# A two-layer fp32 trunk on one core: fp32 output projections, squares and reciprocals on TensorE, down operands summed earlier

## The chip, the core and the metric

The kernel runs on one core of a Trainium2 chip. The core has a matrix engine (TensorE, PE in the profile, with its weight loads as PEld), VectorE (DVE), ScalarE (ACT), GpSimd (POOL) and SyncE (SP, which here issues DMAs); matmuls write to PSUM banks, all other work is between PSUM and SBUF, and DMAs move data to and from DRAM. The metric is the time of one execution on the device in microseconds.

## The reference

Two decoder layers over x of 1024 positions by 1024 features, all in float32. Cut to what matters here:

```python
for layer in range(DEPTH):
    h = rms_norm(x, norm_g)
    # layer 0: 8 MLA heads (softmax) and 8 stick-breaking heads; layer 1: 16 forgetting-attention heads (softmax)
    x = x + (even_mixer(h, positions, *mp) if layer % 2 == 0 else odd_mixer(h, *mp))   # ends in merge_heads(o) @ w_o
    x = x + swiglu(rms_norm(x, f_norm), w_gate, w_up, w_down)

def rms_norm(x, g):
    return x * lax.rsqrt(jnp.mean(x * x, axis=-1, keepdims=True) + EPS) * g
def swiglu(h, w_gate, w_up, w_down):            # 1024 -> 2816 -> 1024
    return (jax.nn.silu(h @ w_gate) * (h @ w_up)) @ w_down
```

Each softmax divides a head's weighted sum of values by the sum of its weights.

## The kernel before

Activations lie transposed, 128 features by 1024 positions (two halves, hf, of 512). **A large product is done in blocks of 2 x 2** by Winograd's form of Strassen's scheme: seven products, taken in the order 1, 6, 5, 7, 2, 4, 3 (`ORDER`), of sums of the four weight blocks (A) with sums of the four activation blocks (X: X11, T2, T1, X12', X21, T4, X22). `pair` (L252) does one pair of 128-row output blocks over nk blocks of the contracted dimension. It loads four raw weight tiles, makes the sums S1 to S4 on POOL (`gadd`, L165), and splits each operand in two fp32r parts: `split` (L153) copies the high part on ACT (L155) and subtracts on DVE to get the low part (L156, or L159 with a sign). Each fp32 product of one block is then three fp32r matmuls, high x high, high x low, low x high, all 128 x 128 weights on 128 x 512. `xadds`/`xsplit` (L232 to L250) make the X sums on POOL and split them, into tiles named xo.

The seven products go to PSUM banks ba, bb, bc. They come back in three ways: product by product with a copy r1 (L321) and two sums U2, U3 (L323, L326); **product by product with an accumulator** (`acc`, L298: nine DVE adds of a bank into an SBUF tile); or **k by k** (`kmajor`, L335, its matmuls at L342), which starts as soon as the first X block is there and needs the weights of all products at once.

**The stages of a layer.** The normalized input's projection; attention head by head (`Heads`, scores St, exponentials p, products with values O at L995); output projection `out_proj` (L1114, four pairs of nk = 4, p = 0 k by k and 1 to 3 with accumulators); eleven gate and eleven up pairs (`ffn`, L1144); down in chunks of 3, 3, 3 and 2 blocks with four pairs each.

**End of attention.** `finish` (L1001) evacuates O: 64 rows of values to a tile o, row 64 (the weights' sum) to a tile dn by ACT (L1012). The reciprocals of each pair of heads go by DMA on POOL's queue: dn to DRAM (rd), back as 128 columns (rc), reciprocal on DVE (L1026), to DRAM (rr), back broadcast to 64 rows (rb), then a multiply on POOL (`scale`, L1035). `out_x` (L1101) loads the heads' results as X of the output projection; for the last pair it uses o where it lies.

**Norms.** `absorb` (L374) takes the outputs of a projection or of down, scales them by the next norm's gain, prepares them as X of the next stage and sums their squares: for the norm in front of the gate/up of layer 0 and others by adds on DVE (L162), or, for those in `PESQ` = (0, 16), by fp32 matmuls with a column block of 64 ones into one bank (L413).

**FFN.** `fu` (L1167 to L1177) multiplies up by the gate's result s, on POOL for three of four tiles, and writes s to DRAM (hS, four writes of 256 KB a pair of blocks). For down, `hadds` loads them (two tiles hld of 512 KB per block), makes the X sums on POOL and splits them; the first two of chunk 0 (`PRE`) are made before the last up pair.

The program is written in this order, and each engine takes its instructions in order; the order on each engine is decided when the program is built, from due times within fixed rings of buffers (`BUFS`: b4 28, T 6, wo 5, raw 6, S 3). SP issues nearly all loads and stores, so a store that waits for its data holds the loads behind it.

Of the kernel before, what the change touches and what calls it, by code (L numbers as in the profile page):

```python
# [19 lines left out]
P = 128  # L20
T = 1024
# [15 lines left out]
PRE = 2  # L37
FGT = 7
LATE = (0,)
PESQ = (0, 16)  # L40
# [37 lines left out]
class Heads:  # L78
# [10 lines left out]
    def run(self, t):  # L89
# [38 lines left out]
class Trunk:  # L128
# [123 lines left out]
    def pair(self, w, nk, X, evac, first=None, acc=None):  # L252
# [20 lines left out]
        for n in ORDER:  # L273
            t = self.tl("hl" if first and n in ORDER[5:] else "wo", "wo", (P, 2, 4, P), F32R)
# [17 lines left out]
        if acc is not None:  # L292
            r = {}

            def plus(ti, hf, bank):
                if (ti, hf) not in r:
                    r[ti, hf] = acc(ti, hf)
                nc.vector.tensor_tensor(r[ti, hf], bank, r[ti, hf], ALU.add)  # L298
            prod(1, ba, True)
            plus(1, 1, ba)  # L300
            plus(1, 0, ba)
            plus(0, 1, ba)
            prod(6, bb, True)
            plus(0, 1, bb)
            prod(5, bc, True)
            plus(1, 1, bc)
            prod(7, bb, False)
            plus(1, 1, bb)
            evac(1, 1, r[1, 1])
            prod(2, ba, False)  # L310
            plus(0, 0, ba)
            evac(0, 0, r[0, 0])
            prod(4, bb, False)
            plus(1, 0, bb)
            evac(1, 0, r[1, 0])
            prod(3, bc, False)
            plus(0, 1, bc)
            evac(0, 1, r[0, 1])
            return
# [15 lines left out]
    def kmajor(self, A, X, ks, evac, r1, U2, U3):  # L335
# [3 lines left out]
        for m, k in enumerate(ks):  # L339
            for n in ORDER:  # L340
                for i, (a, b) in enumerate(((0, 0), (0, 1), (1, 0))):
                    nc.tensor.matmul(bank[n], A[n][:, a, k], X[n, k][:, b], start=m == 0 and i == 0,  # L342
                                     stop=m == len(ks) - 1 and i == 2, skip_group_check=True)
# [1022 lines left out]
```

## Time and profile before

| | us |
|---|---|
| median of 3 runs (lowest, highest) | 2813.67 (2801.68, 2820.46) |
| the profiled execution | 2817.3 |
| its span, first to last instruction | 2815.5 |
| PE busy in the span | 2622.2 |
| DVE / POOL / ACT busy | 2179.3 / 1587.7 / 1367.4 |
| mean granted clock of TensorE | 0.964 |

By time: attention of layer 0 ends about 645 us, its output projection runs to 778, gate and up to 1185, down to 1475; in layer 1 the projection lies from 1997 to 2152 and down from 2559 to the end. A matmul record is one pass as the profiler lists it; a native fp32 matmul shows as two. Busy times of an engine are the time in which at least one of its instructions ran; an engine's idle time is put down to what ended it.

### The profile page before, as it was taken

How to read it: one execution, taken by the hardware profiler on the slowest of the kernel's cores; microseconds unless marked ns; L12 is line 12 of the kernel's file. 1: busy time of each engine (PE TensorE's matmuls, PEld its weight loads, DVE VectorE, ACT ScalarE, POOL GpSimd, SP SyncE). 2: the span in 40 equal slices, each digit the busy share in tenths (PEclk: the TensorE clock that was granted, in tenths of full speed). 3: DMA queues.
4: the chain of work that ended last, by engine and by line, in shares of the span. 5: the costliest groups of instructions: out<-in, count | busy, mean ns of one | idle time of the engine just before them, and what ended most of it. 6: DMA issues, size and time to landing. Idle time of an engine off the chain costs nothing.

```text
span 2815.5 us, 35148 instructions
## 1 busy us (share of the span) xinstructions
PE 2622.2 (93%) x11422; PEld 1963.0 (70%) x11422; DVE 2179.3 (77%) x3063; ACT 1367.4 (49%) x2640; POOL 1587.7 (56%) x1355
## 2 busy tenths in 40 slices
PE   7999998997899999998999998999789999998889
PEld 3775554765678888776758866666567888886667
DVE  8777777886965555788899887999799555558987
ACT  5437775673533332343367753777544333333333
POOL 5545665135576666876565533122556666678763
PEclk9999997998999999999999999999899999999999
DMA  3466645624232222242233437666242322224222
GB/s 116 162 203 196 197 148 151 160 84 143 86 98 89 85 77 86 89 149 87 76 109 125 144 123 223 151 176 181 94 133 67 108 86 75 86 77 163 90 90 90
DMA packets 166511, 343.38 MB, mean 122 GB/s; under 512 B 20524, under 2 KB 43904, under 8 KB 166328
## 3 DMA queue, kind: packets, MB, share of 16 engines
q1 hardware_dynamic: 160888, 329.21, 37.9%
q0 software_dynamic: 5056, 11.84, 1.4%
q8 instruction: 90, 1.47, 0.2%
q14 instruction: 93, 0.76, 0.1%
q10 hardware_dynamic: 384, 0.10, 0.0%
HBM read 232.96 MB, written 108.09 MB: 121 GB/s over the span
## 4 chain that ended last, share of the span: by engine, by line
PE 63%; DVE 17%; issue 5%; ACT 5%; DMA 4%; POOL 2%; SPq 0%; DVEq 0%; ACTq 0%; POOLq 0%
PE bb L289 19%; PE bc L289 13%; PE ba L289 13%; PE O L995 5%; DVE xo L156 5%; PE St L974 4%; PE P L342 3%; DVE wo L156 3%; PE Sm L948 2%; DVE acc L298 1%; DVE R L1079 1%; DVE p L985 1%; ACT xo L155 1%; PE psu L659 1%; PE Sz L1069 1%
## 5 line engine op out<-in xcount | busy, mean ns | idle before, releaser
L289 PE MATMUL bb<-xo,wo 128*128 128x512 f32 x2970 | 746.8, 398 | 13.0 <-DVE U L323 4.6
L289 PEld LDWEIGHTS bb<-xo,wo 128*128 128x128 f32 x2970 | 560.9, 190 | 155.3 <-DVE U L323 6.6
L289 PE MATMUL ba<-xo,wo 128*128 128x512 f32 x1980 | 518.6, 406 | 38.3 <-DVE acc L298 19.8
L289 PE MATMUL bc<-xo,wo 128*128 128x512 f32 x1980 | 499.3, 398 | 11.9 <-ACT sq L409 9.4
L289 PEld LDWEIGHTS ba<-xo,wo 128*128 128x128 f32 x1980 | 381.8, 194 | 140.2 <-issue 19.1
L289 PEld LDWEIGHTS bc<-xo,wo 128*128 128x128 f32 x1980 | 373.0, 189 | 107.8 <-ACT sq L409 10.2
L155 ACT ACTIVATE wo<-S 128x512 fp32r<-128x512 f32 (+2 forms) x416 | 241.5, 586 | 413.0 <-PE bb L289 128.4
L156 DVE TENSOR_TENSOR wo<-S,wo 128x512 fp32r<-128x512 f32 (+2 forms) x416 | 381.0, 919 | 72.8 <-ACT wo L155 71.4
L165 POOL TENSOR_TENSOR S<-raw 128x512 f32<-128x512 f32 (+2 forms) x208 | 292.3, 1406 | 111.8 <-DVE wo L156 93.5
L342 PE MATMUL P<-xo,wo 128*128 128x512 f32 x966 | 270.6, 425 | 67.9 <-DVE xo L156 26.0
L995 PE MATMUL O<-p,v 128*65 128x512 f32 (+3 forms) x1152 | 302.4, 364 | 7.9 <-ACT p L984 4.2
L342 PEld LDWEIGHTS P<-xo,wo 128*128 128x128 f32 x966 | 189.7, 202 | 142.5 <-DVE xo L156 39.4
L165 POOL TENSOR_TENSOR S<-raw,S 128x512 f32<-128x512 f32 (+2 forms) x104 | 133.2, 1281 | 272.6 <-issue 153.8
L165 POOL TENSOR_TENSOR s<-s,rs 128x512 f32<-128x512 f32 x156 | 234.5, 1512 | 76.5 <-DVE wo L156 45.3
L155 ACT ACTIVATE wo<-raw 128x512 fp32r<-128x512 f32 (+2 forms) x208 | 121.8, 586 | 312.3 <-PE bb L289 187.4
L156 DVE TENSOR_TENSOR wo<-raw,wo 128x512 fp32r<-128x512 f32 (+2 forms) x208 | 197.8, 951 | 34.0 <-ACT wo L155 34.0
L995 PEld LDWEIGHTS O<-p,v 128*65 128x65 f32 x1152 | 146.9, 142 | 71.5 <-ACT p L155 11.0
L985 DVE TENSOR_TENSOR p<-E,p 128x512 fp32r<-128x512 f32 (+2 forms) x288 | 182.3, 651 | 18.3 <-ACT p L984 16.3
L981 ACT ACTIVATE E<-St 128x512 f32<-128x512 f32 (+2 forms) x288 | 147.4, 518 | 96.4 <-PE St L978 67.0
L156 DVE TENSOR_TENSOR xo<-T,xo 128x512 fp32r<-128x512 f32 x138 | 152.3, 1119 | 42.2 <-ACT xo L155 41.8
L953 DVE TENSOR_REDUCE M<-Sm 128x1 f32<-128x512 f32 (+3 forms) x288 | 152.6, 549 | 26.1 <-PE Sm L951 16.3
L165 POOL TENSOR_TENSOR S<-S,raw 128x512 f32<-128x512 f32 (+2 forms) x104 | 137.7, 1324 | 21.2 <-issue 7.7
(297 smaller groups left out, 4191.6 us busy)
## 6 DMA issues: line engine op xcount, KB each, us to landing
hS<-s SPq DMA_DIRECT2D x88, 256.0 KB
hld<-hS SPq DMA_DIRECT2D x44, 512.0 KB
raw<-in_w1in_dram SPq DMA_DIRECT2D x48, 256.0 KB
Q<-fq SPq DMA_DIRECT2D x48, 256.0 KB
K<-fk SPq DMA_DIRECT2D x48, 256.0 KB
raw<-in_w0g_dram SPq DMA_DIRECT2D x44, 256.0 KB
raw<-in_w0u_dram SPq DMA_DIRECT2D x44, 256.0 KB
raw<-in_w1g_dram SPq DMA_DIRECT2D x44, 256.0 KB
```

The lines of the kernel that those rows point to most:

```text
L155: nc.scalar.activation(hi, src, AF.Copy)
L156: nc.vector.tensor_tensor(lo, src, hi.bitcast(F32), ALU.subtract)
L165: return self.nc.gpsimd.tensor_tensor(o, a, b, op)
L289: nc.tensor.matmul(bank, A[n][:, a, k], X[n, k][:, b], start=first and m == 0, stop=m == 3 * nk - 1, skip_group_check=True)
L298: nc.vector.tensor_tensor(r[ti, hf], bank, r[ti, hf], ALU.add)
L342: nc.tensor.matmul(bank[n], A[n][:, a, k], X[n, k][:, b], start=m == 0 and i == 0, stop=m == len(ks) - 1 and i == 2, skip_group_check=True)
L948: nc.tensor.matmul(S[:, 0:e1 - c0], lhs[:, i * P:(i + 1) * P], rhs[:, c0:e1], start=True, stop=not diag, skip_group_check=True)
L953: nc.vector.tensor_reduce(M[:, m:m + 1], S[:, 0:n], AX.X, ALU.max)
L974: nc.tensor.matmul(S[:, o:H], k[:, j * P:(j + 1) * P], q[:, s:(hf + 1) * H], start=m == 0, stop=m == n - 1 and not diag, skip_group_check= ...
L981: nc.scalar.activation(E[:, o:H], S[:, o:H], AF.Exp)
L985: nc.vector.tensor_tensor(pl[:, o:H], E[:, o:H], ph[:, o:H].bitcast(F32), ALU.subtract)
L995: nc.tensor.matmul(a["O"][hf][0:VW, o:H], v[:, l], p[:, o:H], start=j == 0 and m == 0, stop=last and m == 2, skip_group_check=True)
```

## The change

Five edits.

1. The output projections use `pair32`: no operand is split, each block product is one native fp32 matmul (112 per layer). `out_x` makes its four X sums on POOL and keeps them as they are.
2. For the last two heads of layer 0's softmax heads and of layer 1's, `divide` takes the reciprocals' place over DRAM: four fp32 matmuls turn the row dn into a column block pt, DVE takes reciprocals of 128 x 4, four fp32 matmuls spread them over 64 rows (rb), and DVE multiplies. It is done for each of two heads and two halves.
3. `PESQ` is (0, 8, 16, 24): all norms sum their squares by matmul.
4. In `ffn`, the X sums T1, T2, T4 and X12' of down are made on POOL behind each up pair, and all seven operands are written to DRAM, 256 KB each. Down loads each operand (hx) in product order and splits it; all its pairs use accumulators, none goes k by k. Of `fu`'s three multiplies on POOL two move to DVE. `PRE` is gone.
5. `NAT` = (1,): product 1 of down is native fp32, with A11 and X11 unsplit.

```diff
-PRE = 2
+NAT = (1,)
-PESQ = (0, 16)
+PESQ = (0, 8, 16, 24)
...
+            for k in range(nk if n in nat else 0):
+                nc.tensor.matmul(bank, A[n][:, k], X[n, k], start=first and k == 0, stop=k == nk - 1,
+                                 skip_group_check=True)
...
+        if a["s"].keep and a["h"] >= a["s"].n - 2:
+            return self.divide(a, O, o[r:r + 64], a["dn"][64:65, cols])
...
+    def divide(self, a, O, o, dn):
+        nc = self.nc
+        pt = self.bank("pt", (P, 4), ring="sm")
+        for b in range(4):
+            nc.tensor.matmul(pt[:, b:b + 1], dn[:, b * P:(b + 1) * P], self.one[64:65, 0:1], start=True, stop=True,
+                             skip_group_check=True)
+        rc = self.tl("rd", "rc", (P, 4))
+        nc.vector.reciprocal(rc, pt)
+        rb = self.bank("rb", (64, H), ring="sm")
+        for b in range(4):
+            nc.tensor.matmul(rb[:, b * P:(b + 1) * P], rc[:, b:b + 1].broadcast_to([P, 64]), self.ident, start=True,
+                             stop=True, skip_group_check=True)
+        nc.scalar.copy(o, O[0:64])
+        nc.vector.tensor_tensor(o, o, rb, ALU.mult)
...
-        self.xprep(X, i, q[0], q[1])
+        (X11, X12), (X21, X22) = q
+        t = self.tl("b4", "T12", (P, 2, H))
+        T4 = self.tl("b4", "T4", (P, 2, H))[:, 0]
+        T1, T2 = t[:, 0], t[:, 1]
+        self.gadd(T1, X12, X11, ALU.subtract)
+        self.gadd(T2, X22, T1, ALU.subtract)
+        self.gadd(X12, X22, X12, ALU.subtract)
+        self.gadd(T4, X21, T2, ALU.subtract)
+        for n, x in ((1, X11), (6, T2), (5, T1), (7, X12), (2, X21), (4, T4), (3, X22)):
+            X[n, i] = x
+
+    def pair32(self, w, X, evac, first=None, acc=None):
...
+        def mm(bank, n, k, start, stop):
+            self.nc.tensor.matmul(bank, A[n][:, k], X[n, k], start=start, stop=stop, skip_group_check=True)
...
-                    u = self.tl("T", "u")
+                    last = (ti, hf) != (1, 1)
+                    u = bank if last else add
                     nc.vector.tensor_tensor(u, bank, add, ALU.add)
-                    self.gadd(s, s, u, ALU.mult)
-                nc.sync.dma_start(hS[2 * i + ti, :, hf * H:(hf + 1) * H], s)
+                    (nc.vector if last else nc.gpsimd).tensor_tensor(s, u, s, ALU.mult)
+                if (ti, hf) != (0, 1):
+                    keep(i, 1 + 2 * ti - ti * (1 - hf), s)
...
+            T1, T2, T4 = [self.tl("T", n) for n in ("T1", "T2", "T4")]
...
+            for n, t in ((5, T1), (6, T2), (7, X12), (4, T4)):
+                keep(i, n, t)
...
-            for i in range(nk):
-                self.xsplit(X, i, early.pop(0) if early else hadds(base + i))
+            for n in ORDER:
+                for i in range(nk):
+                    if n in NAT:
+                        if i % 2 == 0:
+                            two = self.tl("b4", "hx2", (P, 2, H))
+                        X[n, i] = two[:, i % 2]
+                        self.load(X[n, i], hS[base + i, n - 1])
+                    else:
+                        t = self.tl("T", "hx")
+                        self.load(t, hS[base + i, n - 1])
+                        X[n, i] = self.tl("b4", "xo", (P, 2, H), F32R)
+                        self.split(X[n, i][:, 0], X[n, i][:, 1], t)
```

Three places in the order that the edits make. First TensorE at the end of layer 0's attention, behind the last scores, before the change (O: products with values; P: the projection's first pair, three fp32r matmuls to a block):

```order
L978 MATMUL St<-maskkb,identb 128x256
L995 MATMUL O_6212<-p,v 65x512 x4
L995 MATMUL O_6211<-p,v 65x256 x2
L342 MATMUL P_6464<-xo,wo 128x512 x6
L995 MATMUL O_6211<-p,v 65x256
L342 MATMUL P_6466<-xo,wo 128x512 x3
L342 MATMUL P_6465<-xo,wo 128x512 x4
L342 MATMUL P_6466<-xo,wo 128x512
L342 MATMUL P_6465<-xo,wo 128x512 x2
L342 MATMUL P_6466<-xo,wo 128x512 x2
L995 MATMUL O_6212<-p,v 65x512 x2
L342 MATMUL P_6467<-xo,wo 128x512 x6
```

and with it (P at L1172 are native matmuls, one to a block; pt is the divide's):

```order
L1172 MATMUL P_6396<-T_6359,raw 128x512
L1172 MATMUL P_6392<-T_6048,S_6382 128x512
L1172 MATMUL P_6392<-T_6224,S_6382 128x512
L1172 MATMUL P_6392<-T_6358,S_6382 128x512
L1011 MATMUL O_6213<-p,v 65x256 x2
L1172 MATMUL P_6394<-o_6044,S_6383 128x512
L1172 MATMUL P_6394<-o_6220,S_6383 128x512
L1172 MATMUL P_6394<-o_6354,S_6383 128x512
L1011 MATMUL O_6213<-p,v 65x256 x4
L1046 MATMUL pt<-oner,dn 128x1 x4
L1172 MATMUL P_6393<-T_6048,S_6382 128x512
L1172 MATMUL P_6393<-T_6224,S_6382 128x512
```

The products with values now have native matmuls between them whose operands are raw weights and sums, and pt stands behind the last of them.

Second SP ahead of layer 0's down, before (s: results of an up pair, those from s_10263 on of the last; hld: the loads of down's chunk 0 that are still out):

```order
L1177 DMA hS0_7220<-s_10008 128x512
L168 DMA raw_10550<-in_w0d0_dram 128x384
L168 DMA raw_10552<-in_w0d0_dram 128x384
L168 DMA hld_10514<-hS0_7220 128x1024
L168 DMA hld_10516<-hS0_7220 128x1024
L168 DMA raw_10676<-in_w0d0_dram 128x384
L168 DMA acc_10659<-x1_102 128x512
L168 DMA acc_10663<-x1_102 128x512
L168 DMA raw_10678<-in_w0d0_dram 128x384
L168 DMA raw_10680<-in_w0d0_dram 128x384
L168 DMA raw_10682<-in_w0d0_dram 128x384
L1177 DMA hS0_7220<-s_10263 128x512
```

and with the change, from the last up pair's first result on (hx: loads of down's operands):

```order
L1220 DMA hS0_6845<-s_9958 128x512
L172 DMA raw_10364<-in_w0d0_dram 128x384
L1220 DMA hS0_6845<-s_9962 128x512
L172 DMA raw_10468<-in_w0d0_dram 128x384
L1220 DMA hS0_6845<-s_9979 128x512
L172 DMA raw_10470<-in_w0d0_dram 128x384
L1220 DMA hS0_6845<-T1_10141 128x512
L172 DMA hx_10157<-hS0_6845 128x512
L172 DMA hx_10167<-hS0_6845 128x512
L1220 DMA hS0_6845<-T2_10142 128x512
L172 DMA hx_10162<-hS0_6845 128x512
L172 DMA hx_10172<-hS0_6845 128x512
```

All loads of chunk 0 stood ahead of the last up pair's writes; now its first split operands are loaded behind the write of T1, a sum made of that pair's results.

Third DVE in down of layer 0, shortly ahead of the start of a chunk, before (xo: operand splits of the next chunk, wo: weight splits, acc: accumulates):

```order
L298 TENSOR_TENSOR acc_10967<-bb,acc_10967 128x512
L156 TENSOR_TENSOR xo<-hld,xo 128x512
L156 TENSOR_TENSOR wo<-S_10927,wo 128x384
L156 TENSOR_TENSOR xo<-hld,xo 128x512
L156 TENSOR_TENSOR xo<-T_11069,xo 128x512
L298 TENSOR_TENSOR acc_10962<-bc,acc_10962 128x512
L156 TENSOR_TENSOR xo<-T_11067,xo 128x512
L156 TENSOR_TENSOR xo<-hld,xo 128x512
L156 TENSOR_TENSOR wo<-raw,wo 128x384
L156 TENSOR_TENSOR xo<-hld,xo 128x512
L298 TENSOR_TENSOR acc_10967<-ba,acc_10967 128x512
L156 TENSOR_TENSOR xo<-T_11072,xo 128x512
```

and with the change:

```order
L331 TENSOR_TENSOR acc_10622<-bb,acc_10622 128x512
L160 TENSOR_TENSOR xo<-hx,xo 128x512
L160 TENSOR_TENSOR wo<-S_10591,wo 128x384
L160 TENSOR_TENSOR xo<-hx,xo 128x512 x2
L331 TENSOR_TENSOR acc_10617<-bc,acc_10617 128x512
L160 TENSOR_TENSOR xo<-hx,xo 128x512 x2
L160 TENSOR_TENSOR wo<-S_10791,wo 128x384
L160 TENSOR_TENSOR xo<-hx,xo 128x512
L331 TENSOR_TENSOR acc_10622<-ba,acc_10622 128x512
L160 TENSOR_TENSOR xo<-hx,xo 128x512
L160 TENSOR_TENSOR wo<-S_10789,wo 128x384
```

In both, the next chunk's operand splits stand between the accumulates of the pair that runs; now they come from hx, in product order.

## Rows read from the trace of the kernel before

**Rows 1.** Page, part 1: busy us (share of the span) xinstructions.

```profile
PE 2622.2 (93%) x11422; PEld 1963.0 (70%) x11422; DVE 2179.3 (77%) x3063; ACT 1367.4 (49%) x2640; POOL 1587.7 (56%) x1355
```

**Rows 2.** Windows: stretch, length, busy (count) of PE PEld DVE ACT POOL, clock, DMA.

```profile
778.00:1185.00 407.00, 402.99 (x1719) 323.37 (x1718) 239.24 (x281) 132.58 (x221) 289.70 (x199) 1.00 0.28 88
818.00:857.00 39.00, 39.00 (x168) 31.37 (x168) 20.93 (x26) 11.99 (x20) 25.90 (x19) 1.00 0.34 108
623.00:778.00 155.00, 124.56 (x474) 94.60 (x474) 130.57 (x158) 72.66 (x130) 89.92 (x62) 0.88 0.34 107
1997.00:2152.00 155.00, 125.00 (x473) 94.20 (x473) 134.03 (x159) 73.63 (x133) 88.35 (x64) 0.88 0.34 107
1185.00:1475.00 290.00, 267.49 (x1070) 200.15 (x1069) 263.23 (x362) 130.11 (x252) 186.89 (x140) 0.97 0.32 105
2559.00:2816.00 257.00, 230.64 (x951) 180.95 (x949) 219.98 (x321) 87.97 (x177) 149.75 (x117) 0.97 0.32 108
1252.00:1321.00 69.00, 61.90 (x256) 48.44 (x255) 61.88 (x84) 25.79 (x51) 44.83 (x33) 0.98 0.28 88
```

**Rows 3.** Chain of waits at 2055 us: start, us, what.

```profile
2059.59 2.80 PE ba L289 x12
2062.39 2.80 PE bb L289 x12
```

**Rows 4.** The same windows' sum over 600:623, 1970:1997, 778:800, 2152:2175.

```profile
sum 95.00, PE 86.70 PEld 64.02 DVE 82.13 ACT 56.35 POOL 57.77; mean PE 21.68 PEld 16.00 DVE 20.53 ACT 14.09 POOL 14.44
```

**Rows 5.** What PE waited for in 623:778: total us, times, longest.

```profile
PE P L342 <- DVE xo L156: 11.1, 4, 4.4
```

**Rows 6.** DVE groups by form: count, busy us, mean ns, idle before.

```profile
L156 DVE TENSOR_TENSOR wo<-S,wo 128x512 fp32r<-128x512 f32 x288 | 283.8, 987 | 68.4 <-ACT wo L155 67.0
...
L156 DVE TENSOR_TENSOR xo<-hld,xo 128x512 fp32r<-128x512 f32 x88 | 83.1, 953 | 0.0
L156 DVE TENSOR_TENSOR wo<-S,wo 128x384 fp32r<-128x384 f32 x96 | 80.5, 844 | 3.0 <-ACT wo L155 3.0
...
L298 DVE TENSOR_TENSOR acc<-ba,acc 128x512 f32<-128x512 f32 x96 | 61.6, 678 | 3.1 <-PE ba L289 3.0
```

**Rows 7.** Timeline of PE at 116 us: start, us, line, operation, count.

```profile
116.46 1.02 PE L492 MATMUL psn<-sqf,oner 128*128 128x512 f32 x2
116.92 2.65 PE L289 MATMUL bb<-xo,wo 128*128 128x512 f32 x9
119.41 1.02 PE L492 MATMUL psn<-sqf,oner 128*128 128x512 f32 x2
```

**Rows 8.** Timeline of PE at 1460 us, squares.

```profile
1460.09 1.07 PE L413 MATMUL pmr<-sq,oner 128*64 128x512 f32 x2
1461.10 1.90 PE L342 MATMUL P<-xo,wo 128*128 128x512 f32 x7
1462.92 1.08 PE L413 MATMUL pmr<-sq,oner 128*64 128x512 f32 x4
1463.93 1.43 PE L342 MATMUL P<-xo,wo 128*128 128x512 f32 x5
```

**Rows 9.** Timeline of PE at 229 us, small fp32 matmuls.

```profile
229.79 0.60 PE L1095 MATMUL Sa<-cst,A 128*128 128x128 f32 x4
```

**Rows 10.** Chain of waits, reciprocals of layer 1.

```profile
2020.25 3.47 DMA rd<-dn
...
2024.30 2.09 DMA rc<-rd
...
2030.01 5.26 DMA rb<-rr
```

**Rows 11.** Tile hld: duration ns min/median/max, first and last start.

```profile
L156 DVE TENSOR_TENSOR xo<-hld,xo x88: 670/678/1805, 1164.0 to 2769.5; 128x512 fp32r<-128x512 f32 x88
L168 SPq DMA_DIRECT2D hld<-hS x44: 319/327/433, 806.8 to 2720.7; - x44
L165 POOL TENSOR_TENSOR T<-hld x22: 1282/1607/1766, 1148.7 to 2725.2; 128x512 f32<-128x512 f32 x22
```

More of the change, by code (lines that the diff above doesn't have):

```diff
@@ L250, in xsplit, with pair @@
             self.split(t[:, 0], t[:, 1], s)
[L252 removed]
+    def pair(self, w, nk, X, evac, first=None, acc=None, nat=()):
         nc = self.nc
@@ L292, in pair @@
         if acc is not None:
[L293 to L319, printed above, removed]
+            return self.nmajor(prod, evac, acc)
+        ba, bb, bc = [self.bank(n, ring=n) for n in ("ba", "bb", "bc")]
         prod(1, ba, True)
@@ L333, in pair, with nmajor, plus, kmajor @@
         evac(0, 1, bc, U2)
-    def kmajor(self, A, X, ks, evac, r1, U2, U3):
+    def nmajor(self, prod, evac, acc):
+        nc = self.nc
+        ba, bb, bc = [self.bank(n, ring=n) for n in ("ba", "bb", "bc")]
+        r = {}
+        def plus(ti, hf, bank):
+            if (ti, hf) not in r:
+                r[ti, hf] = acc(ti, hf)
+            nc.vector.tensor_tensor(r[ti, hf], bank, r[ti, hf], ALU.add)
+        prod(1, ba, True)
+        plus(1, 1, ba)
+        plus(1, 0, ba)
+        plus(0, 1, ba)
+        prod(6, bb, True)
+        plus(0, 1, bb)
+        prod(5, bc, True)
+        plus(1, 1, bc)
+        prod(7, bb, False)
+        plus(1, 1, bb)
+        evac(1, 1, r[1, 1])
+        prod(2, ba, False)
+        plus(0, 0, ba)
+        evac(0, 0, r[0, 0])
+        prod(4, bb, False)
+        plus(1, 0, bb)
+        evac(1, 0, r[1, 0])
+        prod(3, bc, False)
+        plus(0, 1, bc)
+        evac(0, 1, r[0, 1])
+    def kmajor(self, mm, ks, evac, r1, U2, U3):
         nc = self.nc
@@ L340, in kmajor @@
             for n in ORDER:
-                for i, (a, b) in enumerate(((0, 0), (0, 1), (1, 0))):
-                    nc.tensor.matmul(bank[n], A[n][:, a, k], X[n, k][:, b], start=m == 0 and i == 0,
-                                     stop=m == len(ks) - 1 and i == 2, skip_group_check=True)
+                mm(bank[n], n, k, m == 0, m == len(ks) - 1)
         nc.scalar.copy(r1, bank[1])
@@ L1139, in out_proj @@
             if p == 0:
-                self.pair(w[p], 4, X, f, first=order)
+                self.pair32(w[p], X, f, first=order)
             else:
-                self.pair(w[p], 4, X, done, acc=start)
+                self.pair32(w[p], X, done, acc=start)
             self.absorb(e, p, [[got[t, h] for h in range(2)] for t in range(2)])
```

70 lines of the change are left out of this document (44 added, 26 removed).

## Prediction

> **What bounds the kernel now.** I start on the page: TensorE (PE) is busy 93% of the span, no other engine over 77% [rows 1]. Time can be won only by taking matmul time away or by filling the 7%, and the windows by stage say where that is. In the gate and up stage PE is busy 402.99 of 407 us, and one steady pair of 39.00 us holds 168 matmul records [rows 2]. The chain of waits, in a stretch where PE is the chain, gives 2.80 us for 12 of these records, 0.2333 us each [rows 3]; 168 x 0.2333 = 39.2 us, so nothing is lost there, and VectorE (DVE) and GpSimd (POOL) have room. I apply the same price to the other stages of [rows 2], as window minus records x 0.2333: output projection of layer 0 155 - 474 x 0.2333 = 44.4 us lost, of layer 1 155 - 473 x 0.2333 = 44.6, down of layer 0 290 - 1070 x 0.2333 = 40.4, down of layer 1 257 - 951 x 0.2333 = 35.1 (about 6 of it the output's tail, an estimate). Together 164 us, the whole prize. It counts a lower granted clock (0.88 in the projections, 0.97 in down) as lost; I take it to come back with the idle time around it. The last 23 to 27 us of both attentions and the first 22 of both FFNs add 95.00 - 86.70 = 8 us of plain idle time [rows 4].
>
> The waits name who holds PE in the projection: above all the fp32r operands xo from DVE [rows 5]. In down DVE is busy 263 of 290 us [rows 2], and most of that is operand splits: one takes 0.84 to 0.99 us on average, an accumulate out of PSUM 0.68 [rows 6].
>
> **What the change adds to PE.**
> Native fp32: 224 matmuls in the two projections and 88 in down take the place of three fp32r records each (0.70 us). The trace has native matmuls of the same shape, the norm's psn: from 116.46 to 119.41 us there are 2.95 us, with nine fp32r records inside, 2.95 - 9 x 0.2333 = 0.85 [rows 7]. So 312 x (0.85 - 0.70) = 47 us. Bounds: 0.70 (nothing) and the 1.01 us of the squares below (97 us). I take 0.85, as it has the shape.
> Squares: 32 sums move from DVE to TensorE. One square holds PE from 1460.09 to 1461.10, 1.01 us; two side by side from 1462.92 to 1463.93, again 1.01 [rows 8]. By the order the squares stand in 48 such lots after and 24 before: 24 us more. Eight fp32r records of the norms go, 8 x 0.2333 = 2. Net 22 us.
> Divides: eight in the program, each 8 tiny fp32 matmuls, 16 records. A small fp32 record takes 0.15 us [rows 9]: 2.4 us each, 19 in all. Bounds 1 us (were they to overlap) and 3.5 (a wait for the copy and the reciprocal in each), 8 to 28.
> Sum: 47 + 22 + 19 = 88 us more matmul time. The change pays only if it wins back more than 88 of the 164 and 8.
>
> **What it wins.**
> Projections. All operand splits go (28 of X and 28 of the weights per layer), and with them most of DVE's 131 us in 155 [rows 2]. The reciprocals' way over DRAM, 15 us from the issue of rd to the landing of rb [rows 10], becomes a copy, a reciprocal and 8 matmuls on PE's own queue. By the order, natives with operands that are ready (raw weights, POOL sums of earlier head pairs) stand between the last PV products, so PE can run on. Late next: pt, which waits for the last PV and the copy of dn; behind it the multiply and POOL's four sums on that result (1.28 us each at the least [rows 11], two in line before product 6); and the norm's chain at the FFN's start, which stays. I leave 8 us of each 44.5 and win 73; bounds 60, were the POOL sums the bound at each step, and 81.
> Ends of attention and first pairs: 8 us, since natives and squares can stand in the gaps.
> Down. Per chunk of three, DVE drops three X splits of 21 and four weight splits of 28, 3 x 0.95 + 4 x 0.84 = 6.2 us, and gains two accumulates (9 in the place of 7 at the first pair), 1.4 us: from 62 us in one chunk [rows 2] to 57, while PE's work is 4 x (18 x 0.70 + 3 x 0.85) = 60.6. POOL loses 12 sums and 4 accumulates per chunk, so the splits, whose least time is 0.67 us and whose longest 1.81 [rows 11], should come nearer the first. Inside a chunk DVE is then no longer last. What stays is the starts. In layer 0 the first operands of chunk 0 stand on SP behind the writes of the last gate/up pair, T1's among them, and T1 needs the last evacuation; before, they came early. I count an add and a multiply of 0.68 us, T1's 1.6, two issues of 0.33 [rows 11], the landing, and a split on two engines of 0.68 each: 5.0 us and the landing, for which the nearest rows are 2.09 and 5.26 [rows 10]: 7 to 10, and I take 9. Two chunk boundaries cost 3 each: by the order DVE has 18 X splits, 19 weight splits and 27 accumulates in the three pairs ahead of one, at 0.85, 0.7 and 0.68 us 47 us against PE's 45.5. The last chunk, where absorb shares DVE, 7. So 22 of 40.4 stay and 18 are won. Layer 1: 9, 6, 3 for its last chunk and the output's 6, 24 of 35.1; won 11.
> Gate and up. POOL gets four sums a pair, loses two multiplies and, once, the eight sums of the early X: with 1.6 us for each [rows 11], 290 + 10 x 2 x 1.6 - 8 x 1.6 = 309 us of 407; DVE gets two multiplies of 0.68 a pair, 14 us on 239. Seven writes of 256 KB a pair for four are 0.75 MB in 39 us, 20 GB/s on 108, at a DMA share of 0.34 [rows 2]. PE hides all of it: price 0. Without that cover the two extra POOL operations cost their 3.2 us a pair, 70 in both layers.
> Won: 73 + 8 + 18 + 11 = 110. Net -22: 2817.3 - 22 = 2795 against the profiled execution's own time, which lies 3.6 us above the median of the runs; on the median's level **2792 us**.
>
> **The rivals.**
> Faster: the waits in down all but vanish, because DVE falls well under PE. For it: 57 us or fewer against 60.6, with POOL half empty. Against it: by the order, DVE makes the splits just ahead of their use, between accumulates. Only 9 us at each start and the output's 6 stay, so down wins 31 + 20 = 51 and the projections their 81: 51 + 81 + 8 = 140, 30 more than above, 2762.
> Slower: native fp32 runs like the squares, 1.01 us instead of 0.85. For it: [rows 8] is fp32 too. Against it: [rows 7] has the right shape. 312 x 0.16 = +50: 2842. From 0.92 on the 22 us are gone.
> Same, late operands: hx comes late at each chunk, through SP's order and the six buffers of T, so down wins nothing: +29, 2821.
> Same, four passes: a native matmul costs four fp32r records, 0.93 us: 312 x 0.08 = +25, 2817. [rows 7] shows less, so it gets little. The Trainium skill, "FP8 and Floating Point Precision", TensorE Precision Notes, counts four passes through the array for true FP32. By that rule it would be this rival; the trace, with 0.85, does not quite agree.
>
> **How the numbers follow.** Chances: the forecast 0.43 (own range 2776 to 2808), the faster rival 0.29, late operands 0.14, fp32 at 1.01 0.10, four passes 0.04. The range has to take in both sides: 2750 (the faster rival with divides at 1 us each, -11) to 2826 (late operands, with a divide a little longer); the case of 1.01 and the edges are left out. A measurement of this kernel can tell about 1%, 2785.5 and 2842. Faster: 0.29 and 0.12 of the forecast's own spread, 0.41. Slower: 0.10. Same: the rest, 0.49.
>
> **What would show it.** In the profile of the changed kernel: native matmuls of 0.85 us in the projections and in product 1 of down; a projection's stretch near 155 - 36 + 17 (112 natives) + 10 (four divides) = 146 us, and a clock near 1.0 in it; no operand split between the last scores and the FFN; gate/up at 39.2 us a pair; DVE under 90% in down and PE waiting, at a chunk's start alone, for xo<-hx. The forecast is wrong if natives take 1.0 us or more, if PE's idle time in the projections moves to pt or to POOL's sums, or if a gate/up pair grows past 39.2 us behind POOL or SP.

## The result and the profile after

The changed kernel takes 2768.51 us (median of 4 runs, 2766.75 to 2771.89) against 2812.99 us (4 runs): ratio 0.9836, 95% interval 0.9815 to 0.9858. It is 44.5 us faster. The direction was forecast, and the time lies in the range, but the forecast gain was 22 us, half of that. The forecast's faster rival, 2762 us, came closer.

The head of the page and the busy times, which answer to [rows 1]:

```profile
span 2767.6 us, 34820 instructions
...
PE 2666.8 (96%) x11294; PEld 1902.7 (69%) x11294; DVE 1990.3 (72%) x2925; ACT 1290.6 (47%) x2476; POOL 1412.3 (51%) x1263
```

PE is now busy 96% of a shorter span, although it has more matmul time to do. The windows by stage, in the columns of [rows 2] (for each layer the last 30 us of attention and the projection behind the last products with values; gate and up of layer 0; one steady pair; and from the last gate pair's Silu on the two downs, which have most of the last up pair in them):

```profile
612.00:642.00 30.00, 28.06 (x120) 17.07 (x119) 11.11 (x15) 10.73 (x25) 17.27 (x16) 0.89 0.43 141
642.00:766.00 124.00, 123.33 (x337) 57.98 (x337) 62.92 (x87) 44.70 (x74) 51.39 (x38) 1.00 0.29 90
1960.00:1990.00 30.00, 24.67 (x116) 14.57 (x115) 13.04 (x18) 11.55 (x26) 18.08 (x16) 1.00 0.45 141
1990.00:2114.00 124.00, 123.33 (x336) 57.88 (x336) 62.08 (x87) 44.57 (x74) 51.55 (x38) 1.00 0.28 90
766.00:1166.00 400.00, 400.00 (x1723) 324.14 (x1721) 243.87 (x291) 125.96 (x208) 303.25 (x210) 1.00 0.33 103
810.00:849.00 39.00, 39.00 (x169) 31.61 (x169) 22.88 (x28) 12.01 (x20) 28.06 (x20) 1.00 0.32 101
1166.00:1453.00 287.00, 275.87 (x1057) 195.16 (x1056) 238.31 (x360) 127.57 (x240) 111.16 (x93) 0.98 0.47 150
...
2514.00:2768.00 254.00, 239.43 (x928) 176.63 (x926) 192.29 (x314) 85.19 (x163) 73.87 (x69) 0.97 0.49 157
```

Behind the last products with values DVE is busy 63 of 124 us, the clock is 1.00, and PE is busy 123.33 of 124 (before, in a window that starts earlier, DVE had 131 of 155 us and the clock was 0.88). What is still lost lies ahead of that, at the end of attention: PE is busy 28.06 and 24.67 of 30 us there. Gate and up hold PE for all of 400 us with POOL at 303 (309 was worked out). In down DVE fell from 263 of 290 us to 238 of 287 (the window before starts 4 us later in the last up pair).

What PE waits for from 620 to 770 us, to be held against [rows 5]:

```profile
PE O L1011 <- DVE p L1001: 1.2, 1, 1.2
PE O L1011 <- ACT p L1000: 0.8, 1, 0.8
PE pt L1046 <- ACT dn L1028: 0.7, 1, 0.7
```

No operand split is left in it: 2.7 us in all, of which 0.7 is the divide's wait for the copy of dn. In layer 1, from 1960 to 2114 us, there is one more, for POOL's sums:

```profile
PE P L1172 <- POOL T L169: 3.0, 2, 2.5
```

And in down of layer 0:

```profile
PE bb L302 <- ACT xo L159: 7.5, 2, 7.1
PE P L291 <- DVE acc L331: 1.4, 1, 1.4
PE bc L302 <- ACT xo L159: 1.0, 1, 1.0
```

One wait of 7.1 us is most of it, for the first split operands of chunk 0.

To see where the 48 us between the two spans (2815.5 and 2767.6) come from, I cut each profiled execution at points that every kernel here has: the first score matmul of layer 1, the last accumulate of layer 0's down, and the first and the last Silu of a layer (the first and the last gate pair's, so that the last up pair falls to down). All kernels run below stand in the same table, in us:

| kernel | start to gate, layer 0 | gate/up | down | layer 1 in | attention and projection, layer 1 | gate/up | down and tail |
|---|---|---|---|---|---|---|---|
| before | 777.5 | 403.3 | 275.4 | 292.6 | 403.2 | 403.2 | 260.4 |
| changed | 766.1 | 400.1 | 267.4 | 290.0 | 390.6 | 400.1 | 253.3 |
| squares on DVE | 754.0 | 406.3 | 268.3 | 289.0 | 380.9 | 404.7 | 251.3 |
| no native in down | 768.6 | 400.2 | 276.0 | 286.9 | 390.4 | 400.2 | 253.5 |
| split projections | 768.7 | 397.0 | 268.4 | 288.8 | 394.4 | 395.4 | 252.3 |
| no divide | 753.9 | 399.6 | 267.2 | 292.1 | 389.2 | 400.1 | 251.2 |
| split and DRAM | 776.5 | 398.3 | 267.7 | 289.1 | 402.3 | 397.1 | 251.7 |
| old FFN | 767.2 | 405.1 | 277.4 | 293.2 | 393.0 | 405.1 | 258.2 |
| no squares, no divide | 751.8 | 401.5 | 270.3 | 292.4 | 382.8 | 401.5 | 252.2 |
| native projections alone | 745.6 | 406.5 | 275.1 | 294.0 | 374.2 | 406.4 | 260.3 |
| native in chunk 0 only | 768.1 | 400.1 | 274.8 | 291.0 | 395.1 | 400.1 | 251.7 |
| before, no early X | 773.7 | 396.6 | 284.4 | 292.1 | 402.6 | 396.6 | 267.4 |
| sums on POOL's queue | 767.4 | 400.1 | 273.6 | 293.5 | 389.8 | 400.1 | 255.3 |
| three edits kept | 749.8 | 402.3 | 271.3 | 293.5 | 378.6 | 401.4 | 256.0 |

A difference of a few us in one cell says little. Up to some 600 us the changed kernel and those of runs 4, 7, 8 and 12 have one order of instructions on every compute engine, yet their profiled executions come to the same matmul between 598 and 605 us; layer 1 in, which no edit touches, spreads over 7 us. By the table, the change brought 11 and 12.5 us in the two attentions with their projections, 3 in each gate/up, 8 in down of layer 0 and 7 in the last stretch.

The cells also don't hold the same work: at its first Silu the kernel before has 24 matmul records of the first up pair behind it, the changed kernel none. So a second cut goes by PE's own work. "Projection" runs from the 451st product with values of layer 0, or the 501st of layer 1, which lie ahead of the first native matmul, to the 201st fp32r record of gate and up; "middle" from there to the 1751st of their 1848; "last up pair" on to the 1813th. In us, layer 0 / layer 1:

| kernel | projection | middle of gate/up | last up pair |
|---|---|---|---|
| before | 229.5 / 204.6 | 361.7 / 361.7 | 18.9 / 18.7 |
| changed | 225.5 / 198.2 | 360.2 / 360.2 | 15.7 / 15.7 |
| squares on DVE (run 1) | 220.4 / 192.8 | 361.7 / 360.2 | 15.8 / 15.7 |
| split projections (3) | 224.3 / 196.9 | 361.7 / 360.2 | 15.8 / 15.7 |
| no divide (4) | 217.1 / 190.0 | 360.2 / 360.2 | 15.7 / 15.7 |
| split and DRAM (5) | 229.0 / 204.5 | 361.7 / 360.2 | 15.8 / 15.7 |
| old FFN (6) | 225.4 / 201.0 | 360.2 / 360.2 | 18.6 / 18.7 |
| no squares, no divide (7) | 210.1 / 181.8 | 360.2 / 360.2 | 15.7 / 15.7 |
| native projections alone (8) | 210.2 / 181.6 | 360.2 / 360.2 | 18.7 / 17.4 |
| before, no early X (10) | 229.9 / 202.8 | 360.2 / 360.2 | 14.4 / 14.4 |

Where down has native products, two of them stand in the last up pair's stretch (15.7 for 14.4). The middle, 1550 records in one order, takes one of two times, 233.3 or 232.4 ns a record, at a granted clock of 1.00 in both; what decides between them is not known. It is worth 1.5 us in each layer.

### The profile page after: what moved, and what is told of

Same layout as the page of the kernel before. It is cut to its first block, busy times and chain, and to the rows that moved or that the text cites. A ratio compares the mean times of both kernels' runs of the same rounds, so it can differ in the third digit from the quotient of the medians.

```text
span 2767.6 us, 34820 instructions
## 1 busy us (share of the span) xinstructions
PE 2666.8 (96%) x11294; PEld 1902.7 (69%) x11294; DVE 1990.3 (72%) x2925; ACT 1290.6 (47%) x2476; POOL 1412.3 (51%) x1263
## 4 chain that ended last, share of the span: by engine, by line
PE 81%; DVE 8%; DMA 3%; ACT 3%; issue 3%; POOL 1%; SPq 0%; DVEq 0%; ACTq 0%; POOLq 0%
PE bb L302 23%; PE bc L302 15%; PE ba L302 13%; PE O L1011 6%; PE St L990 4%; PE ba L298 2%; PE bb L1172 2%; PE P L291 2%; PE P L1172 2%; PE Sm L964 2%; PE ba L1172 2%; PE bc L1172 2%; DVE xo L160 1%; PE pmr L429 1%; DVE wo L160 1%
## 5 line engine op out<-in xcount | busy, mean ns | idle before, releaser
L302 PE MATMUL ba<-xo,wo 128*128 128x512 f32 x1704 | 431.7, 397 | 3.8 <-ACT r L309 2.3
L159 ACT ACTIVATE wo<-S 128x512 fp32r<-128x512 f32 (+2 forms) x384 | 222.3, 583 | 419.7 <-PE bb L302 185.5
L160 DVE TENSOR_TENSOR wo<-S,wo 128x512 fp32r<-128x512 f32 (+2 forms) x384 | 354.0, 924 | 64.5 <-ACT wo L159 63.4
L302 PEld LDWEIGHTS ba<-xo,wo 128*128 128x128 f32 x1704 | 320.1, 188 | 85.1 <-issue 3.7
L169 POOL TENSOR_TENSOR s<-s,rs 128x512 f32<-128x512 f32 x156 | 248.5, 1600 | 15.1 <-ACT s L1227 14.9
L159 ACT ACTIVATE wo<-raw 128x512 fp32r<-128x512 f32 (+2 forms) x160 | 96.3, 602 | 257.4 <-PE bb L302 152.3
L1001 DVE TENSOR_TENSOR p<-E,p 128x512 fp32r<-128x512 f32 (+2 forms) x288 | 180.5, 645 | 31.4 <-ACT p L1000 28.8
L160 DVE TENSOR_TENSOR wo<-raw,wo 128x512 fp32r<-128x512 f32 (+2 forms) x160 | 151.5, 947 | 17.9 <-ACT wo L159 17.9
L1000 ACT ACTIVATE p<-St 128x512 fp32r<-128x512 f32 (+2 forms) x288 | 147.7, 523 | 1.3 <-ACT mr L975 0.7
L1227 ACT ACTIVATE s<-s 128x512 f32<-128x512 f32 x88 | 55.7, 633 | 139.3 <-POOL s L169 138.5
L160 DVE TENSOR_TENSOR xo<-hx,xo 128x512 fp32r<-128x512 f32 x132 | 92.7, 726 | 26.5 <-ACT xo L159 26.5
## 6 DMA issues: line engine op xcount, KB each, us to landing
hx<-hS SPq DMA_DIRECT2D x154, 256.0 KB
hS<-s SPq DMA_DIRECT2D x88, 256.0 KB
hS<-T SPq DMA_DIRECT2D x66, 256.0 KB
raw<-in_w1in_dram SPq DMA_DIRECT2D x48, 256.0 KB
Q<-fq SPq DMA_DIRECT2D x48, 256.0 KB
K<-fk SPq DMA_DIRECT2D x48, 256.0 KB
raw<-in_w0g_dram SPq DMA_DIRECT2D x44, 256.0 KB
raw<-in_w0u_dram SPq DMA_DIRECT2D x44, 256.0 KB
```

What stands on the lines that cost most here:

```text
L159: nc.scalar.activation(hi, src, AF.Copy)
L160: nc.vector.tensor_tensor(lo, src, hi.bitcast(F32), ALU.subtract)
L169: return self.nc.gpsimd.tensor_tensor(o, a, b, op)
L302: nc.tensor.matmul(bank, A[n][:, a, k], X[n, k][:, b], start=first and m == 0, stop=m == 3 * nk - 1, skip_group_check=True)
L1000: nc.scalar.activation(ph[:, o:H], S[:, o:H], AF.Exp)
L1001: nc.vector.tensor_tensor(pl[:, o:H], E[:, o:H], ph[:, o:H].bitcast(F32), ALU.subtract)
```

## The experiments

Ratios are to the kernel before, run on the same chip; to compare with the changed kernel hold them against its 0.9836. 0.001 is 2.8 us.

**1. Squares of the FFN norms back on DVE.**

```diff
-PESQ = (0, 8, 16, 24)
+PESQ = (0, 16)
```

> The changed kernel with the squares of the two FFN norms back on DVE (PESQ = (0, 16)); all else as changed (2768.5 us). Theory A (PE is the bound of the projections after the change, and each term costs its matmul time): the 24 lots of squares of 1.01 us leave PE and 8 fp32r records of 0.2333 come back, 22 us less: 2746 us. Theory B (the squares filled time in which PE would have waited, so they cost nothing, and the 32 adds of about 1 us on DVE stand at the end of each projection instead): 2768 us or a little more.

Measured 2755.22 us, ratio 0.9789 (0.9768 to 0.9810): 13 us faster than the changed kernel, between the theories and nearer to A. In the table the stretch up to gate falls by 12 and 10 us, as the squares' matmul time says, and gate/up grows by 6 and 5 (1.5 of the 6 is its middle). The waits of PE around the first gate pair there:

```profile
PE bc L302 <- DVE U L365: 2.5, 1, 2.5
PE ba L302 <- ACT wo L159: 1.1, 1, 1.1
```

In the changed kernel PE waits for nothing between 766 and 1166 us. So the squares' matmul time was priced right, and about half of it is won back from waits at the first gate pair, which the sum didn't have. That it is an earlier norm that ends these waits fits the edit, but wasn't tested apart. It still is a loss of 13 us.

**2. No native product in down.**

```diff
-NAT = (1,)
+NAT = ()
```

> The changed kernel with product 1 of down back in fp32r (NAT = ()): 88 native matmuls of 0.86 us become 264 fp32r records of 0.2333 us, 88 more operand splits on ACT and DVE. Theory A (PE bounds down and the natives cost what their matmul time says): 88 x 0.157 = 14 us less, 2755 us. Theory B (the natives pay their way: they need no split, so they fill the wait at the first chunk's start, 7 us in each layer, and spare DVE the splits): the gain goes back to waits, 2765 to 2775 us.

Measured 2778.13 us, ratio 0.9866 (0.9848 to 0.9883): slower than the changed kernel and 3 us above theory B's range, so theory A fell. PE has 7 us less to do in each layer, and it goes back to waits, in layer 0 with interest (down 276.0 for 267.4):

```profile
PE ba L302 <- ACT xo L159: 8.8, 2, 7.1
PE bb L302 <- DVE acc L331: 3.3, 5, 0.9
PE P L291 <- ACT wo L159: 1.5, 1, 1.5
PE P L291 <- DVE wo L163: 1.0, 1, 1.0
```

The wait at the start is as long as with the native product, 7.1 us, so the first half of theory B (the native fills the start) isn't shown; the small waits on DVE and ACT behind it are new. Which chunk gains is asked in run 9.

**3. Output projections back in fp32r with splits, the divides kept.** `out_x` and `out_proj` are those of before; the last pair's result lies in two single tiles, as before.

```diff
-                if self.keep and g == n - 2:
+                if False:
...
-                self.pair32(w[p], X, f, first=order)
+                self.pair(w[p], 4, X, f, first=order)
...
-                self.pair32(w[p], X, done, acc=start)
+                self.pair(w[p], 4, X, done, acc=start)
```

> The changed kernel with the output projections back in fp32r with splits, the divides on chip kept (their result in two single tiles as before). Theory A (the operand splits on DVE were what the projections lost 44 us on per layer; the changed kernel lost some 3): 224 x 0.157 = 35 us of matmul time less, and 2 x 38 to 41 us of waits back: 2809 to 2815 us. Theory B (the reciprocals' way over DRAM was the larger part of the loss, and that stays removed): about half of the waits come back, 40 us, and 35 go: 2770 to 2775 us.

Measured 2773.87 us, ratio 0.9853 (0.9832 to 0.9875). Theory B's time, and within the intervals the same as the changed kernel. With the chain over DRAM gone, the splits alone hold PE up little in the projection itself. Its windows at the end of attention and in the projection:

```profile
600.00:650.00 50.00, 38.22 (x171) 27.22 (x171) 31.38 (x45) 28.55 (x60) 21.05 (x18) 0.76 0.25 84
650.00:769.00 119.00, 117.26 (x481) 84.15 (x479) 93.99 (x122) 61.45 (x106) 65.05 (x43) 1.00 0.33 109
```

What is left of the loss sits at the end of attention (38.22 of 50 us at a clock of 0.76); behind it PE is busy 117.26 of 119. It isn't small: with 35 us less to do, PE needs as long as in the changed kernel.

**4. Reciprocals of the last pair back over DRAM, native projections kept.**

```diff
-        if a["s"].keep and a["h"] >= a["s"].n - 2:
+        if False:
             return self.divide(a, O, o[r:r + 64], a["dn"][64:65, cols])
```

> The changed kernel with the last pair's reciprocals back over DRAM. Theory A (the native matmuls of the first three blocks, 21 of 0.86 us or 18 us, cover most of the 15 us chain; the eight divides cost about 2 us each): 8 x 2 = 16 us less PE time, and 0 to 10 us of wait per layer back: 2755 to 2775 us. Theory B (the chain is bare, since the first pair needs the last block's sums early): 15 us and three POOL sums per layer come back, 35 to 40 us, less 16: 2787 to 2792 us.

Measured 2756.09 us, ratio 0.9791 (0.9769 to 0.9812): theory A, 12 us faster than the changed kernel. By the second cut its projections are 8.4 and 8.2 us shorter, about the matmul time of four divides in each layer. The chain of 15 us ([rows 10]) is nearly covered by native matmuls whose operands are ready; in layer 0 this is all that PE waits for from 600 to 755 us:

```profile
PE P L1172 <- POOL T L169: 4.6, 2, 4.0
```

**5. Both undone: splits, and reciprocals over DRAM.** The edits of 3 and 4 together.

> The changed kernel with both the fp32r output projections and the reciprocals over DRAM back, so only the squares and the FFN's edits stay. Theory A (either edit alone takes away the projections' loss, since the chain over DRAM and the splits hurt only together: the last block's sums come late and then still have to be split): the loss of before returns in both layers. 2815 less some 24 us for gate, up and down, plus 5 to 15 us of squares: 2796 to 2806 us. Theory B (the two edits act independently, so undoing both adds up): 2774 + 2756 - 2768 = 2762 us.

Measured 2783.95 us, ratio 0.9884 (0.9862 to 0.9906). Neither time: 12 below A's range, 22 above B's. The table shows that A's mechanism holds: start to gate is 776.5 us and attention with projection 402.3 in layer 1, within 1 us of before, so the long time is back in full; the squares, 11 us more in each, stand in its waits and cost nothing. The long waits are, as before, for operand splits:

```profile
PE P L287 <- DVE xo L156: 6.8, 3, 4.2
PE P L287 <- ACT xo L155: 6.5, 2, 6.3
```

A's time was off because I set the FFN's gain at 24 us (run 6 gives 33) and the squares at 5 to 15. So the two edits overlap. With splits, the divide on chip wins 10 us (2784 to 2774); with native operands it loses 12 (2756 to 2768). With the chain over DRAM, native operands win 28 us (2784 to 2756); with the divide, 5, which is within the intervals.

**6. The FFN of before, all else as changed.** The whole of `ffn`, `PRE` = 2, down in fp32r.

```diff
-                self.pair(I[f"w{l}d{c}"][p], nk, X, done, acc=start, nat=NAT)
+                if p == 0:
+                    self.pair(I[f"w{l}d{c}"][p], nk, X, f, first=tuple(range(nk)))
+                else:
+                    self.pair(I[f"w{l}d{c}"][p], nk, X, done, acc=start)
```

> The changed kernel with the FFN of before (X sums of down made in down, four loads of each block, first pair k by k, all products of down in fp32r). Theory A (the FFN's edits bring what the traces of before and after differ by, some 3 us in gate and up and 7 to 10 in down of each layer): 20 to 26 us more, 2788 to 2794 us. Theory B (the gain there is the native product's alone, or comes from what precedes): 2768 to 2778 us.

Measured 2801.02 us, ratio 0.9954 (0.9937 to 0.9970): 32.5 us above the changed kernel, more than A. Five us in each gate/up, 10 and 5 in the downs and 3 in layer 1 in (within its spread) make 28 in the profiled spans. In gate and up the longest wait of before is back, at the last up pair:

```profile
PE ba L303 <- ACT r L310: 2.6, 1, 2.6
```

The FFN's edits are worth 33 of the 44.5 us; the forecast had them at 16 (29 won in down, less 13 for the natives). Without squares and divides they are worth 25 (run 8 to run 7). Which of them brings down's share (the sums made ahead, accumulators in the place of k by k, or `fu`'s multiplies on DVE) was not tested apart.

**7. No squares and no divide.** The edits of 1 and 4.

> The changed kernel with the squares of the FFN norms on DVE and the last reciprocals over DRAM; native projections and the FFN's edits stay. Theory A (squares and divides are matmul time in a stage that PE bounds, their undoing adds up): 2755 + 2756 - 2768 = 2743 us. Theory B (the 12 us that each gave back came out of the same waits at the end of attention): 2753 to 2757 us.

Measured 2750.31 us, ratio 0.9773 (0.9750 to 0.9797), the fastest of all and below both kernels. It lies between the theories: adding up runs 1 and 4 would be 2743. In the stretches where the two edits work they add up in full: by the second cut the projections of both layers are 32 us shorter than the changed kernel's, for 10 in run 1 and 17 in run 4. What is missing lies elsewhere, above all early in layer 1's attention, which is 10 us longer up to the 501st product with values (7 longer in run 4). There PE waits for loads of Q (from 1716 to 1816 us; the changed kernel waits 0.6 us for them):

```profile
PE St L990 <- DMA Q<-mr: 3.3, 1, 3.3
PE Sm L964 <- DMA Q<-rows: 3.1, 1, 3.1
```

What delays these loads was not tested, and the intervals are 13 us wide.

**8. The kernel before with native projections alone.**

```diff
-                self.pair(w[p], 4, X, f, first=order)
+                self.pair32(w[p], X, f, first=order)
...
-                self.pair(w[p], 4, X, done, acc=start)
+                self.pair32(w[p], X, done, acc=start)
```

> The kernel before with the native output projections alone. Theory A (native operands need no split, so the chain over DRAM is covered by the native matmuls of the first three blocks and nearly all of the 44 us per layer come back, against 35 us of matmul time in both): 2815 - 2 x 40 + 35 = 2770 us, less up to 8 us at the ends of attention, 2762. Theory B (the chain stays bare for the last block): half of that, 2790 us.

Measured 2775.26 us, ratio 0.9857 (0.9834 to 0.9880): 38 us for this edit alone, nearer to theory A. (`pair32` and `out_x` are the changed kernel's. Its profiled execution was the fastest of its five, 10 us under the median, so its row in the table flatters it.) PE pays 35 us of matmul time for it, so it regains some 73 us. From 612 to 746 us PE waits for 8 us in all, mostly for POOL's sums of the last block:

```profile
PE P L1173 <- POOL T L170: 4.9, 2, 3.9
```

**9. Native product in chunk 0 only.**

```diff
-                    if n in NAT:
+                    if n in NAT and c == 0:
...
-acc=start, nat=NAT)
+acc=start, nat=NAT if c == 0 else ())
```

> The changed kernel with product 1 of down native in the first chunk alone (24 of the 88 native matmuls stay). Without any native product down of layer 0 was 8.6 us longer, though its matmul time is 7 us shorter. Theory A (the native product pays at the start of chunk 0 alone, where its operands need no split and fill the wait for hx): that is kept, and 64 x 0.157 = 10 us of matmul time go: 2758 us. Theory B (it pays in every chunk, by the splits that DVE and ACT are spared): the waits on DVE of the run without native products come back in the later chunks, 2770 to 2778 us.

Measured 2781.88 us, ratio 0.9890 (0.9869 to 0.9910): theory A fell, the start isn't where it pays. Cut by the accumulates, the four chunks of layer 0 take 85.8, 63.4, 56.6 and 61.6 us in the changed kernel, 91.8, 61.1, 57.7 and 65.3 without natives, 91.6, 60.4, 57.7 and 65.1 here. The first two must be taken together, since matmuls of chunk 1 stand ahead of chunk 0's last accumulate: PE's first 250 records behind the last Silu come within 0.4 us of each other here and in the changed kernel. Together they take 149.2 us in the changed kernel, 152.9 without natives and 152.0 here. So each of these sums is longer without natives, by 1 to 4 us, though chunks 1 and 2 have 4 us less matmul time each: theory B's mechanism, as the small waits on DVE and ACT of run 2 say. In layer 1 the last chunk, without absorb's splits beside it, is 3 us shorter instead (38.6 for 41.7). The downs make 6 of the 13 us; the rest lies in stretches that this edit leaves alone, and stays unexplained.

**10. The kernel before without the early X.**

```diff
-PRE = 2
+PRE = 0
```

> The kernel before with PRE = 0: no X sums and splits of down's first two blocks ahead of the last up pair. Theory A (these early splits, which fill DVE from 1170 to 1180 us, hold up the last pair's evacuation and cost gate and up 3 to 5 us in each layer): gate and up fall from 403 to 399 us, but down's start is bare and loses what the early loads saved, 5 to 10 us: 2813 to 2825 us. Theory B (the early X cost nothing): gate and up stay at 403, and the time grows by 10 to 20 us.

Measured 2818.20 us, ratio 1.0021 (1.0009 to 1.0033), as theory A said: gate/up fall by 6.7 us in each layer, and down pays 9 and 7. In the kernel before, DVE has no gap where these splits are made, and the gate pair's evacuation is late. Of before, one window, and PE's longest wait in gate and up, which ends in it; of the kernel without early X, the same place:

```profile
1170.00:1180.00 10.00, 7.41 (x28) 5.67 (x27) 10.00 (x11) 3.98 (x8) 8.77 (x6) 0.89 0.40 120
```

```profile
PE ba L289 <- ACT r L321: 2.6, 1, 2.6
```

```profile
1158.00:1172.00 14.00, 14.00 (x62) 11.34 (x61) 8.46 (x9) 5.21 (x9) 11.85 (x10) 1.00 0.22 66
```

Without the early X PE is full there and DVE busy 8.46 of 14 us. By the second cut the last up pair's stretch falls from 18.9 to 14.4 us (the wait, and matmuls at a lower clock behind it), the middle by 1.5. So the early X cost some 4.5 us in each layer, a cost of before that the forecast had not seen and that the change takes away.

**11. The last block's sums written by POOL's queue.**

```diff
-            nc.sync.dma_start(hS[i, n - 1], t)
+            (nc.gpsimd if i == 10 and n in (4, 5, 6, 7) else nc.sync).dma_start(hS[i, n - 1], t)
```

> The changed kernel with the last block's four sums written to DRAM by POOL's DMA queue in the place of SP's, so that the loads of chunk 0's first operands do not stand behind the write of T1. Theory A (SP's order makes the wait of 7 us for xo at the start of down): it falls to 1 to 4 us, 3 to 6 us less in each layer, 2757 to 2763 us. Theory B (the wait is the landing and the split themselves, or the buffers of T): no change, 2768 us.

Measured 2780.87 us, ratio 0.9888 (0.9869 to 0.9907): slower, and the wait is there unchanged.

```profile
PE bb L302 <- ACT xo L159: 7.1, 1, 7.1
PE bc L302 <- ACT xo L159: 3.6, 1, 3.6
```

But the edit did not do what it should. SP's timeline at the start of down, of this kernel and then of the changed one (their last Silus are 1.3 us apart):

```profile
1186.33 0.33 SPq L172 DMA_DIRECT2D acc<-x  x1
1186.71 1.37 SPq L172 DMA_DIRECT2D hx<-hS  x3
```

```profile
1184.99 0.33 SPq L1220 DMA_DIRECT2D hS<-T  x1
1185.37 0.92 SPq L172 DMA_DIRECT2D hx<-hS  x2
```

The first loads of hx are issued 19.2 us behind the last Silu in both. In the changed kernel the write of T1 stands ahead of them; here it is a load of acc, and from 1184 to 1187.6 us SP waits for the same sum on POOL before it:

```profile
SPq L172 <- POOL T L169: 1.5, 1, 1.5
```

So nothing came earlier, and what an earlier issue would do to the wait stays open. What the trace of the changed kernel does show is the time behind it: until 1226 us the DMA engines are full with chunk 0's operands, of which seven to a block are now loaded.

```profile
1188.00:1196.00 8.00, 6.72 (x13) 3.84 (x13) 3.97 (x6) 3.46 (x6) 0.75 (x1) 0.50 1.01 377
1196.00:1206.00 10.00, 8.93 (x34) 6.05 (x34) 8.59 (x15) 6.48 (x13) 2.79 (x3) 0.96 0.93 308
1206.00:1226.00 20.00, 19.83 (x77) 14.06 (x76) 19.64 (x31) 6.71 (x13) 5.64 (x6) 1.00 0.99 334
```

**12. Native projections and FFN edits, squares on DVE, reciprocals over DRAM, and the edit of 11.**

> Native projections and the FFN's edits, squares of the FFN norms on DVE, last reciprocals over DRAM, and the last block's sums written by POOL's queue. Theory A (what the runs so far showed adds up): 2750 us of the kernel without squares and divides, less 6 to 12: 2738 to 2744 us. Theory B (the sums' writes on POOL delay POOL's own adds): 2750 us or more.

Measured 2755.17 us, ratio 0.9796 (0.9775 to 0.9817): theory B, no better than run 7. It is 5 us above run 7, where run 11 was 12 above the changed kernel, so what that edit costs is not settled.

## Why the prediction was off by half

**What held.** PE was the bound and the sum of matmul time was right, 87 us for the 88 worked out. A native matmul takes 0.857 us, for the 0.85 worked out; the chain of waits in down shows eight records, four matmuls, in 3.43 us:

```profile
1169.18 0.86 PE ba L298 x2
1170.04 2.78 PE bb L302 x12
1172.82 3.43 PE ba L298 x8
```

That settles two rivals: 1.01 us a matmul, and the price of four fp32r records (0.93). The Trainium skill ("FP8 and Floating Point Precision", TensorE Precision Notes) counts four passes for true FP32; at 0.2333 us a pass that would be 0.93 us, an estimate, and the rows show less. A lot of squares takes 1.00 us (from 701.90 to 702.90, with 24 us more in all), and a divide holds PE for 0.98 us of pt and 1.01 of rb, 2.0 for the 2.4 taken, plus a wait of 0.67:

```profile
701.90 1.07 PE L429 MATMUL pmr<-sq,oner 128*64 128x512 f32 x2
702.90 1.98 PE L1172 MATMUL bb<-o,S 128*128 128x512 f32 x4
```

```profile
642.69 1.05 PE L1046 MATMUL pt<-oner,dn 1*128 1x1 f32 x8 [0.67 <-ACT dn L1028]
643.67 3.70 PE L1172 MATMUL P<-T,S 128*128 128x512 f32 x8
647.30 1.09 PE L1052 MATMUL rb<-cst,rc 128*64 128x128 f32 x8
648.31 1.13 PE L1172 MATMUL P<-o,raw 128*128 128x512 f32 x2
```

Gate and up hid POOL's extra sums, and down's start waits 7 us for its first operands (9 were taken; whether SP's order makes them is open, run 11).

**What failed: the price 0 of gate and up.** By the second cut, both layers together, in us, rounded (won: what the stretch lost in length and the matmul time added in it):

| stretch of PE's work | before | changed | matmul time added | won | forecast |
|---|---|---|---|---|---|
| projections, with the ends of attention and the first gate and up | 434.1 | 423.7 | 73 | 84 | 81 |
| middle of gate/up | 723.3 | 720.4 | 0 | 3 | 0 |
| last up pair | 37.6 | 31.4 | 3 | 10 | 0 |
| down | 533.0 | 514.1 | 10 | 29 | 29 |
| all else, the same matmul work in both | 1087.6 | 1077.9 | 0 | 10 | 0 |
| sum | 2815.5 | 2767.6 | 87 | 135 | 110 |

- The projections and down came out nearly as worked out. That 8 us of each 44.5 stay was about right: 642 to 766 us loses next to nothing, but the end of attention does (the windows from 612 and 1960 us above).
- Gate and up gave 13 us and were put at nothing. "PE hides all of it: price 0" asked only what the change adds there. That the stage lost nothing before, its first 22 us apart, was read off one steady pair, though [rows 2] have 4 us of it idle: at its end the early X held up the last pair by 4.5 us in each layer (runs 6 and 10). The sum has the end of these splits only as a loss at down's start. The other 3 us are the spacing of the middle's records.
- 10 us lie in stretches whose matmul work is the same in both kernels. That is within what executions of one order differ by, and 3 to 4 of it come from the choice of execution: the profiled one of before is 4.3 us above its median, that of the changed kernel 0.9. The sum has no term for this, and what it is stays open.

So the profiled spans miss the forecast's 22 us by 26, the medians by 22: about half of it is the term for gate and up, the rest is not clear of the spread between executions. One reading in the prediction was off as well: down's 40.4 us in layer 0 price 32 records of squares at 0.2333 us, where 12 lots of 1.00 us stand, so 5 of it were work.

The faster rival, 2762 us, came closest by luck: it won 81 and 8 us in the projections, where 84 came, and 51 in down, where 29 did. DVE fell under PE there, 238 of 287 us, but the starts stayed.

**What the sum didn't separate.** It gave the projections' 73 us to the native operands and the divide as one. Set against run 5, which has neither, and with the matmul time that each adds (35 us for the natives, 16 for the divides), the divide alone wins back 26 us of waits (run 3), the natives alone 63 (run 4) and both 66. So the natives take away nearly all of the loss; beside them the divide covers a wait that hardly exists and costs 12 us. That the chain over DRAM hurt because the last block's operands came late and then had to be split fits these four runs and the waits in them, but no run shows it apart. The squares cost 13 us. Without these two edits the change would have been worth 62.7 us (run 7, 2813.01 to 2750.31).

**The natives in down** were put at 13 us of cost. Run 2 shows that taking them out makes the kernel 10 us slower, 9 of them in layer 0's down: the splits that they spare DVE and ACT are worth more there than the 7 us of matmul time. In layer 1 the two cancel. The wait at the start of chunk 0 is as long with them as without.

## What to carry to other kernels

When two edits remove the same wait, price each as if the other were there: here the second one only added its cost. A steady stretch gives a stage's price per matmul, not what the stage loses at its two ends; read these from rows of their own. Work prefetched for the next stage has a price in the stage where it is made; look for an engine that is full just there. And compare stages between places in the bounding engine's work: an event on another engine can lie at different work in two kernels.

## What the runs showed of the hardware

TensorE's granted clock fell to 0.50, the lower of its two levels (1.2 GHz), around the idle 7 us at the start of down (the window 1188 to 1196 above), with 13 matmul records in 8 us, where 34 fit at 0.2333 us each. PE was busy for 6.72 of them; 13 records take 3.0 us at the full clock, so this wait cost some 3 to 4 us more than itself.

A native fp32 matmul with 128 output rows takes 0.857 us, a square with 64 output rows 1.01: the smaller one is the slower, and two of them side by side take no longer than one [rows 8]. Why is not shown.
